# Split weights of `kv0` and of q0's plain blocks kept in DRAM and loaded split in the last quarter

## The chip, the cores and the metric

The kernel runs on one core of one Trainium2 chip. The metric is device time in microseconds (us) of one launch. Three runs of the kernel before the change took 2904.12 us in the median (2902.68 to 2905.22). About 0.2%, some 5.8 us, is what a measurement can tell from no change.

## What is computed

A trunk of two layers over 2048 tokens of width 1024, in float32. Layer A is a gated MLP whose gate mixes tokens inside chunks of 128. Layer B is attention with 24 query heads in three groups of dilation 1, 4 and 16; all read one set of keys and values that is projected from layer A's output. Cut to what the change touches:

```python
h = rms_norm(x, norm_g) * (1 + scale) + shift
k, v = jnp.split(h @ w_kv, 2, axis=-1)          # shared_kv, 6 heads of 128 each
...
qz = h @ w_in                                    # dilated_layer: 24 query heads and z
q = qz[..., :N_Q_HEADS * HEAD_DIM]; z = qz[..., N_Q_HEADS * HEAD_DIM:]
for g, (window, d) in enumerate(DILATED_GROUPS):
    o, lse = dilated_group_attn(q_g, k_g, v_g, slopes_g, window, d)
alpha = jax.nn.softmax(jnp.stack(lses), axis=0)
y = sum(alpha * outs) * jax.nn.silu(z)
return x + gate * (y @ w_out)
```

## The kernel before

The tokens run in four quarters of 512 (`Q` = 0 to 3 in the code). Each goes through layer A and then through `proj_B` (L1205), which projects keys and values in three column blocks (`kv2`, `kv1`, `kv0`) and queries and gate in blocks `q2`, `q1`, `q0`, `z`. Attention is written as generators that are interleaved with the projections as filler: group 2 (dilation 16) needs all tokens, so its 16 blocks run in quarter 4 beside `kv0`, `q1` and `q0`; the last blocks of groups 1 and 0 (blocks 12 to 15) run beside the last product with `w_out`. This product, `pf` (L1678 to L1680), makes 16 tiles of tokens times two halves, 24 matmuls each; its left operand `yb` is made by `prepare` and `make_yb` out of `og` (attention output) and `zt` (gate), both read back from DRAM.

Matmuls run in three terms. Each float32 weight `w` of 128 rows by 512 columns, called a unit, is split into a high and a low half, and the product is `a_hi w_hi + a_hi w_lo + a_lo w_hi` (`mm3`). A unit comes in one of two ways:

- `raw_unit` (L264) loads 256 KB into a buffer of the pool `rp` (six), and `split` makes the high half by an ACT copy (L260) and the low half by a DVE subtraction (L262), in a buffer of the pool `wp` (eight);
- `split_unit` (L273) loads 512 KB, already split, from DRAM straight into a `wp` buffer. Some weights are kept that way already: `wk1`, `wk2` for the even units of `kv1`, `kv2`.

A plain block of a q or z projection is 4 units. In `dense_s` (L536) a projection is seven products of half size, on the blocks "11", "21", "22" (plain columns of the weight) and "t1" to "t4" (sums and differences of blocks, made earlier and kept in `wt`); so each projection has 12 plain units and 16 of the other kind. `kv0` is an ordinary product of 8 units (`kv_units`, L289).

All DMAs are issued by SP in one row, in order, on eight lanes in rotation; an issue waits for the lane's DMA eight before. Stores are put into `pending` and issued by `flush` behind the next units' loads. A scheduler orders the instructions of every engine ahead of time, from its own estimate of times, so that a load or a split that is added or taken away changes the order elsewhere too. Each engine then runs its row strictly in that order.

At the tail, a local attention block `b` of group `g` goes through these steps: keys, values (`kv`, L1337 for the block before, L1338 for its own) and queries (`qt`) are loaded; `pk` and `pq` transpose keys and queries on PE (L1362, L1374); `kT` and `qT` are their copies in a high half (ACT, L1368, L1379) and a low half (DVE, L1369, L1380); `ps` are the scores (L1407 to L1409); DVE adds the bias and takes the maximum (`pr`, `stat`, L1413 to L1417); ACT takes exponentials (L1423); `pp` transposes them (L1465), `pT` is the copy, `po` the output (L1484).

Of the kernel before, what the change touches and what calls it, by code (L numbers as in the profile page):

```python
# [12 lines left out]
F32 = mybir.dt.float32  # L13
# [6 lines left out]
D = 1024  # L20
S = 2048
AW = 2048
NQ = 4
# [11 lines left out]
def trunk(ctx, tc, out, x, c, a_ada_w, a_ada_b, a_norm_g, a_w_in, a_sgu_g, a_w_spatial,  # L35
# [21 lines left out]
    dp = ctx.enter_context(tc.tile_pool(name="dp", bufs=1, space=bass.MemoryType.DRAM))  # L57
# [12 lines left out]

    wq = [dp.tile([D, 512], F32, name=f"wq{i}") for i in range(4)]
    wob = [dp.tile([2, D, 512], F32, name=f"wob{n}") for n in range(2)]
    wk2 = {n: dp.tile([512, 2, 512], F32, name=f"wk{n}") for n in (1, 2)}

    fillers = []
# [206 lines left out]
    def rows_of(t, k):  # L282
        return t[k * P:(k + 1) * P]
# [5 lines left out]
    def kv_units(Q, n, nm):  # L289

        saved = n and Q > 2 - n
        us = []
        for k in range(KT):
            if saved and k % 2 == 0:
                us.append(split_unit(rows_of(wk2[n], k // 2), f"{nm}{k}"))
                continue
            us.append(raw_unit(w_kv[k * P:(k + 1) * P, n * 512:(n + 1) * 512], f"{nm}{k}"))
            if n and Q == 2 - n and k % 2 == 0:
                nc.sync.dma_start(rows_of(wk2[n], k // 2), us[k].bitcast(F32))
        return us  # L300

    last_mm = [None]
# [216 lines left out]
    def v_blocks(b):  # L519

        n0 = AW + b * D
        src = {"11": (a_w_in, 0, n0), "21": (a_w_in, 4, n0), "22": (a_w_in, 4, n0 + 512)}
        src.update({f"t{i + 1}": (wv[b][i], 0, 0) for i in range(4)})
        return src, 4

    late_stores = []

# [677 lines left out]
    def proj_B(Q, hk, hb, keep, tail, ahead):  # L1205
# [41 lines left out]
        def q_block(g):  # L1247
            def ev(t, src, n):
                if t < 2 and n == 0:
                    c_ = sum_tile(f"qc{g}{Q}{t}")  # L1250
                    nc.scalar.activation(c_[:, 0:512], src, AF.Copy)
                    src = c_
                nm = f"q{g}{n}{Q}_{t}"
                sq = evt(f"hs_{nm}")
                nc.scalar.activation(sq, src[:, 0:512], AF.Square)
                nc.vector.tensor_reduce(src[:, 512:516], sq.rearrange("p (h d) -> p h d", d=P),
                                        AX.X, ALU.add)
                pending.append((qd[g][rows(t), n, 0:516], src[:, 0:516]))
            dense_s(hb, in_blocks(g), f"q{Q}{g}", ev)

        def z_block(**extra):
            def ev(t, src, n):
# [497 lines left out]
```

## Time and profile before

| what | value |
|---|---|
| median of three runs | 2904.12 us |
| the profiled execution | 2904.99 us, span 2903.3 us |
| granted TensorE clock, mean | 0.999 |
| PE busy | 2875.6 us, 99% of the span |
| DVE, ACT, POOL busy | 76%, 57%, 9% |
| DMA | 693.82 MB, mean 239 GB/s |

The page gives busy time by engine first, then the span in slices, the DMA queues, the chain that ended last and the costliest groups. The span is the time from the first to the last instruction of the profiled execution; 1.7 us of its own time lie around it. A group's line names code line, engine, operation and tiles, then busy time, mean duration in ns and the idle time ahead of it with what ended it. A timeline's row has the start, the length, the instruction, and in brackets the idle time before it and the engine and instruction that ended it. Matmuls are pipelined: a 128x512 matmul is listed with 0.39 us, but the next starts 0.23 us after it.

### The profile page before, as it was taken

The page shows a single profiled execution, that of the slowest core. Times are in us where ns is not written, and L with a number is a line of the kernel's source. Part 1 is how long each engine was busy: PE and PEld are TensorE (multiplying, and loading weights), DVE is VectorE, ACT ScalarE, POOL GpSimd, SP SyncE. Part 2 cuts the span into 40 slices and gives each one's busy share as a digit, 9 for nine tenths or more (in the row PEclk, how much of TensorE's full clock was granted, in tenths as well). Part 3 has the DMA queues.
Part 4 walks back from the last instruction along what each step waited for, and adds up shares of the span by engine and source line. Part 5 has one row for each costly group of instructions (what it writes and reads, how often), then busy time and mean ns, then how long its engine had stood idle before and what let it go on. Part 6 is the DMA issues. An engine that isn't in the chain of part 4 may idle for free. (4 is left out here: it accounts for less than half of the span.)

```text
span 2903.3 us, 44921 instructions
## 1 busy us (share of the span) xinstructions
PE 2875.6 (99%) x14610; PEld 2419.2 (83%) x14610; DVE 2219.1 (76%) x4246; ACT 1667.6 (57%) x3400; POOL 258.2 (9%) x549
## 2 busy tenths in 40 slices
PE   8999999999999999999999999999999999999999
PEld 5888888888888888888888888888888888988887
DVE  6786677787758986887878876987678876888972
ACT  4423345668456765676555665676355667876540
POOL 1000001101011000000010000000010003311100
PEclk9999999999999999999999999999999999999999
DMA  7899788777998577776676676766554667889842
GB/s 258 298 311 297 265 287 292 241 250 249 311 334 284 171 259 225 239 247 201 212 262 198 192 253 212 243 225 197 172 174 155 223 219 238 269 265 340 260 144 87
DMA packets 390783, 693.82 MB, mean 239 GB/s; under 512 B 42027, under 2 KB 119821, under 8 KB 390549
## 3 DMA queue, kind: packets, MB, share of 16 engines
q1 hardware_dynamic: 390548, 690.97, 72.3%
q8 instruction: 115, 1.88, 0.3%
q14 instruction: 120, 0.98, 0.1%
HBM read 530.97 MB, written 159.85 MB: 238 GB/s over the span
## 5 line engine op out<-in xcount | busy, mean ns | idle before, releaser
L306 PE MATMUL pd_kv<-w_kv,hkh 128*128 128x512 f32 x768 | 238.5, 391 | 0.3 <-DMA w_kv<-wk 0.2
L355 PE MATMUL pd_u<-hAh,w_u 128*128 128x512 f32 x512 | 207.8, 406 | 0.0
L355 PE MATMUL pd_z<-hAh,w_z 128*128 128x512 f32 x512 | 205.8, 402 | 0.0
L1423 ACT ACTIVATE pr<-pr,stat,rt 128x256 f32<-128x256 f32 (+1 forms) x320 | 177.4, 556 | 45.3 <-DVE stat L1420 30.0
L357 PE MATMUL pd_u<-hAh,w_u 128*128 128x512 f32 x512 | 200.6, 392 | 1.7 <-DVE w_u L262 1.7
L357 PE MATMUL pd_z<-hAh,w_z 128*128 128x512 f32 x512 | 200.4, 392 | 0.0
L356 PE MATMUL pd_u<-hAl,w_u 128*128 128x512 f32 x512 | 200.0, 391 | 0.0
L356 PE MATMUL pd_z<-hAl,w_z 128*128 128x512 f32 x512 | 199.8, 390 | 0.0
L306 PEld LDWEIGHTS pd_kv<-w_kv,hkh 128*128 128x128 f32 x768 | 143.3, 188 | 30.1 <-ACT w_kv L260 0.6
L1484 PEld LDWEIGHTS po<-kv,pT 128*128 128x128 f32 x1200 | 147.6, 191 | 7.4 <-ACT pT L1321 1.2
L1484 PE MATMUL po<-kv,pT 128*128 128x128 f32 x1200 | 149.8, 275 | 1.0 <-ACT pT L1321 1.0
L306 PE MATMUL pd_kv<-w_kv,hkl 128*128 128x512 f32 x384 | 149.8, 390 | 0.0
L1351 POOL TENSOR_SCALAR rt<-qt 128x4 f32<-128x4 f32 x96 | 26.8, 279 | 1311.9 <-DMA qt<-qd 724.7
L1413 DVE SCALAR_TENSOR_TENSOR pr<-dist,rt,ps 128x256 f32<-128x256 f32 (+1 forms) x320 | 124.7, 431 | 22.4 <-PE ps L1409 10.4
L260 ACT ACTIVATE w_u<-raw_u 128x512 fp32r<-128x512 f32 x96 | 59.5, 628 | 142.4 <-PE pd_u L357 95.2
L260 ACT ACTIVATE w_o<-raw_o 128x512 fp32r<-128x512 f32 x104 | 64.2, 628 | 96.4 <-PE pd_o L306 37.8
L260 ACT ACTIVATE w_q<-raw_q 128x512 fp32r<-128x512 f32 x144 | 88.6, 628 | 49.9 <-PE pd_kv L306 9.9
L357 PEld LDWEIGHTS pd_u<-hAh,w_u 128*128 128x128 f32 x512 | 96.1, 188 | 23.9 <-DVE w_u L262 2.9
L357 PEld LDWEIGHTS pd_z<-hAh,w_z 128*128 128x128 f32 x512 | 96.1, 188 | 21.0
L355 PEld LDWEIGHTS pd_u<-hAh,w_u 128*128 128x128 f32 x512 | 96.5, 188 | 18.4 <-issue 1.7
L356 PEld LDWEIGHTS pd_z<-hAl,w_z 128*128 128x128 f32 x512 | 96.5, 188 | 17.6
L355 PEld LDWEIGHTS pd_z<-hAh,w_z 128*128 128x128 f32 x512 | 96.4, 188 | 17.4
(866 smaller groups left out, 7944.8 us busy)
## 6 DMA issues: line engine op xcount, KB each, us to landing
raw_q<-in_b_w_in_dram SPq DMA_DIRECT2D x144, 256.0 KB, 3.8
w_z<-wuz SPq DMA_DIRECT2D x64, 512.0 KB, 4.3
raw_o<-in_a_w_out_dram SPq DMA_DIRECT2D x104, 256.0 KB, 3.5
qt<-qd SPq DMA_DIRECT2D x96, 258.0 KB, 3.6
raw_v<-in_a_w_in_dram SPq DMA_DIRECT2D x96, 256.0 KB, 4.0
raw_u<-in_a_w_in_dram SPq DMA_DIRECT2D x96, 256.0 KB, 5.3
od<-ot SPq DMA_DIRECT2D x96, 256.0 KB, 2.5
raw_kv<-in_w_kv_dram SPq DMA_DIRECT2D x76, 256.0 KB, 4.7
```

What stands on the lines that cost most here:

```text
L260: nc.scalar.activation(hi, src, AF.Copy)
L306: last_mm[0] = nc.tensor.matmul(pt, a, u[:, w, :], start=f, stop=e, skip_group_check=more)
L355: nc.tensor.matmul(pts[i], wh, hh[:, k, :], start=k == 0, stop=False)
L356: nc.tensor.matmul(pts[i], wh, hl[:, k, :], start=False, stop=False)
L357: nc.tensor.matmul(pts[i], wl, hh[:, k, :], start=False, stop=k == KT - 1)
L1351: nc.gpsimd.tensor_scalar(rt[:, 12:16], u["qt"][:, 512:516], 1.0 / P, EPS, ALU.mult, ALU.add)
L1413: nc.vector.scalar_tensor_tensor(pr[:, i, :], dist3[:, d0:d0 + w], u["rt"][:, h:h + 1], psc[:, i, :], ALU.mult, ALU.add)
L1423: nc.scalar.activation(pr[:, i, :], pr[:, i, :], AF.Exp, bias=mneg[:, i:i + 1], scale=u["rt"][:, h:h + 1], accum_out=lsum[:, i:i + 1])
L1484: nc.tensor.matmul(po[:, h * P:(h + 1) * P], u["pT"][h // hp][:, h % hp, j, :], u["kv"][:, j, kh, 1, :], start=j == 0, stop=j == nk - 1)
```

## The change

Two kinds of units of the last quarter get a split copy in DRAM. `wk0` holds the eight units of `kv0`: even units are stored in quarter 2, odd ones in quarter 3; even ones are loaded split in quarters 3 and 4, odd ones in quarter 4. `wq0` holds the three plain blocks of `q0`, four units each: "11" is stored in quarter 1, "21" in quarter 2, "22" in quarter 3, and all 12 are loaded split in quarter 4. That makes 20 stores of 512 KB, and 24 loads of 512 KB where there were loads of 256 KB with a split.

```diff
+    wk0 = dp.tile([D, 2, 512], F32, name="wk0")
+    wq0 = {b: dp.tile([512, 2, 512], F32, name=f"wq0{b}") for b in ("11", "21", "22")}
...
         for k in range(KT):
+            if n == 0 and Q > 1 + k % 2:
+                us.append(split_unit(rows_of(wk0, k), f"{nm}{k}"))
+                continue
             if saved and k % 2 == 0:
...
+            if n == 0 and Q == 1 + k % 2:
+                pending.append((rows_of(wk0, k), us[k].bitcast(F32)))
         return us
...
+    def q0_blocks(Q):
+
+        src, nk = in_blocks(0)
+        for i, name in enumerate(("11", "21", "22")):
+            w, k0, n0 = src[name]
+
+            def units(nm, i=i, name=name, w=w, k0=k0, n0=n0):
+                if Q == NQ - 1:
+                    return [split_unit(rows_of(wq0[name], k), f"{nm}{k}") for k in range(nk)]
+                us = wunits(w, k0, n0, nm, nk)
+                if Q == i:
+                    pending.extend((rows_of(wq0[name], k), us[k].bitcast(F32)) for k in range(nk))
+                return us
+            src[name] = units
+        return src, nk
...
-            dense_s(hb, in_blocks(g), f"q{Q}{g}", ev)
+            dense_s(hb, in_blocks(g) if g else q0_blocks(Q), f"q{Q}{g}", ev)
```

The code behind the change has 23 lines more ahead of it, so `L1361` of the changed kernel is `L1338` of the one before. The scheduler's order moves in places far from the edit. Two of them follow.

At the tail, on SP, around the load of the own half of block 12 of group 1 (`kv1_12`; `L1337` and `L1360` load the half of the block before). Before, it stands among the last loads of the weights `z3bt`, ahead of `wo`:

```order
L1337 DMA kv1_12_26308<-kvd_91 128x512 [waits DMAHW7_49,PE_49]
L267 DMA raw_z3bt1_1_26084<-wt3_0_115 128x512 [waits DMAHW0_49,DVE_49]
L267 DMA raw_z3bt1_2_26089<-wt3_0_115 128x512 [waits DMAHW1_49,DVE_49]
L1338 DMA kv1_12_26308<-kvd_91 128x512 [waits DMAHW2_49]
L267 DMA raw_z3bt1_3_26094<-wt3_0_115 128x512 [waits DMAHW3_49,DVE_49]
L1337 DMA kv1_13_26375<-kvd_91 128x512 [waits DMAHW4_49,DVE_49]
```

Now it stands behind the loads of tile 4's `og` and `zt`, which are the last of four tiles' loads, all behind `wo`:

```order
L1621 DMA og4_0_26249<-od0_95 128x1024 [waits DMAHW4_49,PE_49]
L1621 DMA og4_2_26251<-od2_97 128x1024 [waits DMAHW5_49,PE_49]
L1628 DMA zt4_0_26253<-zd_101 128x512 [waits DMAHW6_49,DVE_49]
L1628 DMA zt4_1_26254<-zd_101 128x512 [waits DMAHW7_49,DVE_49]
L1361 DMA kv1_12_26260<-kvd_91 128x512 [waits DMAHW0_49]
L1360 DMA kv1_13_26327<-kvd_91 128x512 [waits DMAHW1_49]
```

The half of the block before has kept its place among the `z3bt` loads; the own half has moved back by some 40 issues.

At the tail, on PE, where block 12's exponentials are transposed (`pp1_12`). Before, its transposes stand among the matmuls of `pf0_1`, the second half of tile 0, and `pk1_12` with the first scores stood ahead, among `pf0_0`:

```order
L1465 MATMUL pp1_12_00_26399<-ident_136,pr1_12_00_26343 128x128 x2
L1679 MATMUL pf0_1_26457<-wo11_26122,yb0_26233 128x512
L1680 MATMUL pf0_1_26457<-wo10_25997,yb0_26233 128x512
L1465 MATMUL pp1_12_00_26399<-ident_136,pr1_12_00_26343 128x128 x2
L1678 MATMUL pf0_1_26457<-wo10_25997,yb0_26233 128x512
L1679 MATMUL pf0_1_26457<-wo11_26122,yb0_26233 128x512
L1465 MATMUL pp1_12_01_26406<-ident_136,pr1_12_01_26357 128x128 x2
L1407 MATMUL ps1_12_10_26424<-kT1_12_26325,qT1_12_1_26390 128x256
```

Now the last matmuls of `pf0_1` come ahead of `pk1_12`, and scores and transposes follow one another:

```order
L1702 MATMUL pf0_1_26409<-wo11_26074,yb0_26185 128x512
L1703 MATMUL pf0_1_26409<-wo10_25949,yb0_26185 128x512
L1385 MATMUL pk1_12_26272<-ident_140,kv1_12_26260 128x128 x3
L1430 MATMUL ps1_12_00_26294<-kT1_12_26277,qT1_12_0_26285 128x256
L1430 MATMUL ps1_12_01_26308<-kT1_12_26277,qT1_12_0_26285 128x256
L1397 MATMUL pq1_12_1_26337<-ident_140,qt1_12_1_26265 128x128 x2
L1431 MATMUL ps1_12_00_26294<-kT1_12_26277,qT1_12_0_26285 128x256
L1432 MATMUL ps1_12_00_26294<-kT1_12_26277,qT1_12_0_26285 128x256
L1430 MATMUL ps1_12_00_26294<-kT1_12_26277,qT1_12_0_26285 128x256
```

and, five rows further on, the transposes of the exponentials:

```order
L1431 MATMUL ps1_12_01_26308<-kT1_12_26277,qT1_12_0_26285 128x256
L1432 MATMUL ps1_12_01_26308<-kT1_12_26277,qT1_12_0_26285 128x256
L1397 MATMUL pq1_12_1_26337<-ident_140,qt1_12_1_26265 128x128 x2
L1488 MATMUL pp1_12_00_26351<-ident_140,pr1_12_00_26295 128x128 x4
L1488 MATMUL pp1_12_01_26358<-ident_140,pr1_12_01_26309 128x128 x2
L1430 MATMUL ps1_12_10_26376<-kT1_12_26277,qT1_12_1_26342 128x256
```

What moved is the filler: all 24 matmuls of `pf0_1` now stand ahead of the chain from `pk1_12` to `pp1_12`, none between its steps.

On DVE the low half of `kT1_12`, which those scores need, stood right behind the two operations of tile 0's `yb`:

```order
L1641 TENSOR_TENSOR yb0_26233<-pyb0_0_26234,yb0_26233 128x512
L1641 TENSOR_TENSOR yb0_26233<-pyb0_1_26241,yb0_26233 128x512
L1369 TENSOR_TENSOR kT1_12_26325<-pk1_12_26320,kT1_12_26325 128x512
L1380 SCALAR_TENSOR_TENSOR qT1_12_0_26333<-pq1_12_0_26328,gqk_544,qT1_12_0_26333 128x512
L262 TENSOR_TENSOR w_z3b22_0_26187<-raw_z3b22_0_26188,w_z3b22_0_26187 128x512
L262 TENSOR_TENSOR w_z3b22_1_26192<-raw_z3b22_1_26193,w_z3b22_1_26192 128x512
```

Now it stands behind the preparation of tiles 1 to 4 (`og`, three operations in two halves a tile), whose last rows are these:

```order
L1708 TENSOR_TENSOR of0_0_26404<-pf0_0_26248,xr10_0_26244 128x512
L1641 TENSOR_TENSOR og3_0_26236<-og3_0_26236,zt3_0_26240 128x512
L1641 TENSOR_TENSOR og3_0_26236<-og3_0_26236,zt3_1_26241 128x512
L1564 TENSOR_TENSOR og4_2_26251<-og4_2_26251,wst_197 128x512 x2
L1640 TENSOR_TENSOR og4_0_26249<-og4_0_26249,og4_2_26251 128x512 x2
L1641 TENSOR_TENSOR og4_0_26249<-og4_0_26249,zt4_0_26253 128x512
L1641 TENSOR_TENSOR og4_0_26249<-og4_0_26249,zt4_1_26254 128x512
L1392 TENSOR_TENSOR kT1_12_26277<-pk1_12_26272,kT1_12_26277 128x512
```

It moved behind 24 of them and one `of`.

In quarter 2, on DVE, at the second product of the gate's projection (`z1b21`; `st_z1bu` takes the first products out of PSUM). Before, three low halves stand ahead of it:

```order
L262 TENSOR_TENSOR w_z1b21_0_11897<-raw_z1b21_0_11898,w_z1b21_0_11897 128x512
L262 TENSOR_TENSOR w_z1b21_1_11902<-raw_z1b21_1_11903,w_z1b21_1_11902 128x512
L262 TENSOR_TENSOR w_z1b21_2_11907<-raw_z1b21_2_11908,w_z1b21_2_11907 128x512
L578 TENSOR_TENSOR st_z1bu0_11835<-pd_z1bb0_11773,st_z1bu0_11835 128x512
L578 TENSOR_TENSOR st_z1bu1_11836<-pd_z1bb1_11774,st_z1bu1_11836 128x512
L262 TENSOR_TENSOR w_z1b21_3_11912<-raw_z1b21_3_11913,w_z1b21_3_11912 128x512
```

Now both evacuations stand ahead of all four:

```order
L601 TENSOR_TENSOR st_z1bu0_11851<-pd_z1bb0_11789,st_z1bu0_11851 128x512
L601 TENSOR_TENSOR st_z1bu1_11852<-pd_z1bb1_11790,st_z1bu1_11852 128x512
L264 TENSOR_TENSOR w_z1b21_0_11913<-raw_z1b21_0_11914,w_z1b21_0_11913 128x512
L264 TENSOR_TENSOR w_z1b21_1_11918<-raw_z1b21_1_11919,w_z1b21_1_11918 128x512
L264 TENSOR_TENSOR w_z1b21_2_11923<-raw_z1b21_2_11924,w_z1b21_2_11923 128x512
L264 TENSOR_TENSOR w_z1b21_3_11928<-raw_z1b21_3_11929,w_z1b21_3_11928 128x512
```

The splits of the next product have moved behind the two evacuations, and on PE the four matmuls that need only high halves (of `w_z1b21_0` and of the product after it) now stand ahead of the others.

## Rows read from the trace of the kernel before

**Rows 1.** The page's first part: busy time of each engine, share, instructions.
```profile
PE 2875.6 (99%) x14610; PEld 2419.2 (83%) x14610; DVE 2219.1 (76%) x4246; ACT 1667.6 (57%) x3400; POOL 258.2 (9%) x549
```

**Rows 2.** What PE waited for, whole run: us in total, times, longest.
```profile
PE pt_a L880 <- DVE x L874: 5.3, 3, 3.3
PE pva L126 <- DMA veca<-in_a_ada_b_dram: 5.0, 1, 5.0
...
PE pp L1465 <- ACT pr L1423: 1.6, 1, 1.6
PE pf L1680 <- DVE yb L1641: 1.4, 1, 1.4
```

**Rows 3.** By stretch: us of PE, PEld, DVE, ACT, POOL; clock, DMA share, GB/s.
```profile
2400.00:2450.00 50.00, 47.20 (x291) 40.01 (x290) 31.24 (x76) 32.61 (x90) 20.99 (x44) 1.00 0.63 198
...
2550.00:2600.00 50.00, 50.00 (x279) 43.38 (x278) 40.96 (x85) 36.58 (x91) 6.88 (x16) 1.00 0.80 261
2600.00:2650.00 50.00, 49.74 (x250) 41.41 (x248) 36.44 (x65) 32.96 (x73) 0.00 (x0) 1.00 0.98 363
...
2700.00:2750.00 50.00, 49.23 (x302) 42.78 (x301) 44.68 (x97) 24.37 (x70) 7.25 (x16) 1.00 0.80 263
```

**Rows 4.** Groups by line, whole run: busy us, mean ns, idle before.
```profile
L262 DVE TENSOR_TENSOR w_q<-raw_q,w_q 128x512 fp32r<-128x512 f32 x144 | 94.4, 685 | 18.6 <-ACT w_q L260 18.0
...
L260 ACT ACTIVATE w_q<-raw_q 128x512 fp32r<-128x512 f32 x144 | 88.6, 628 | 49.9 <-PE pd_kv L306 9.9 <-DMA raw_q<-in_b_w_in_dram 7.4 <-DVE w_q L262 6.6
```

**Rows 5.** PE in time, tail: start, us, instruction, idle before in brackets.
```profile
2624.73 1.03 PE L1638 MATMUL pyb<-ident,og 128*128 128x128 f32 x8
...
2629.25 0.73 PE L306 MATMUL pd_z3ba<-w_z3b,hob 128*128 128x512 f32 x2 [0.23 <-ACT w_z3b L260]
...
2630.41 5.18 PE L306 MATMUL pd_z3ba<-w_z3b,hob 128*128 128x512 f32 x22
```

**Rows 6.** Landing of the loads of `kv`, 2300 to 2600 us.
```profile
DMA to landing us min/median/max: 3.3/4.3/5.2
```

**Rows 7.** Landing of the loads of `zt`, 2640 to 2660 us.
```profile
DMA to landing us min/median/max: 5.6/6.0/6.4
```

**Rows 8.** DVE in time, quarter 2, start of z1.
```profile
1234.27 1.89 DVE L262 TENSOR_TENSOR w_z1b<-raw_z1b,w_z1b 128x512 fp32r<-128x512 f32 x3
1236.17 1.37 DVE L578 TENSOR_TENSOR st_z1bu<-pd_z1bb,st_z1bu 128x512 f32<-128x512 f32 x2
```

**Rows 9.** PE in time, quarter 2, start of z1.
```profile
1231.21 5.60 PE L306 MATMUL pd_z1bb<-w_z1bt,hob 128*128 128x512 f32 x24
```

**Rows 10.** SP's queue in time, tail: start and length of DMA issues.
```profile
2602.36 0.42 SPq L1338 DMA_DIRECT2D kv<-kvd  x1
...
2642.74 0.96 SPq L1605 DMA_DIRECT2D zt<-zd  x2
2644.05 0.32 SPq L1343 DMA_DIRECT2D qt<-qd  x1
```

**Rows 11.** DVE in time, tail.
```profile
2636.24 1.28 DVE L1541 TENSOR_TENSOR og<-og,wst 128x512 f32<-128x512 f32 x2
2637.44 1.28 DVE L1617 TENSOR_TENSOR og<-og,og 128x512 f32<-128x512 f32 x2
...
2639.85 1.26 DVE L1413 SCALAR_TENSOR_TENSOR pr<-dist,rt,ps 128x256 f32<-128x256 f32 x3
...
2642.01 0.15 DVE L1417 SCALAR_TENSOR_TENSOR stat<-rt 128x2 f32<-128x2 f32 x1
```

**Rows 12.** ACT in time, tail.
```profile
2642.24 1.28 ACT L1423 ACT_TABLE_LOAD   x1 [1.55 <-DVE stat L1417]
...
2645.30 0.59 ACT L1423 ACTIVATE pr<-pr,stat,rt 128x256 f32<-128x256 f32 x1
```

**Rows 13.** The same columns for ten us at the program's start.
```profile
20.00:30.00 10.00, 8.90 (x22) 4.28 (x21) 7.80 (x14) 0.81 (x1) 0.00 (x0) 0.66 1.08 356
```

**Rows 14.** PE in time, start of the program.
```profile
17.62 1.84 PE L890 MATMUL pc_a<-sc,aw 128*128 128x1 f32 x16
```

## The prediction

> **What bounds the kernel now.** The table of engines comes first: TensorE (PE) is busy 99% of the span, 2875.6 of 2903.3 us [rows 1], so 27.7 us are all that any change can take away without removing matmuls, and this one removes none. The list of what PE waits for comes next: the two longest, 5.3 and 5.0, lie at the program's start, and what quarter 4 and the tail hold is small: 1.6 us for the exponentials `pr` and 1.4 for the low half of `yb` [rows 2]. None of them is a split of a weight of kv0 or q0. The table by 50-us stretches says the same: PE has 47.20 us in 2400 to 2450, where kv0 of quarter 4 ends and the group-2 attention starts, 50.00 in 2550 to 2600, where q0's blocks run, and 49.74 in 2600 to 2650; DVE (VectorE) and ACT (ScalarE) are far from full there, 31 to 41 and 33 to 37 of 50 [rows 3]. So this kernel is bound by PE's instruction stream, and what counts is whether PE's in-order row of instructions still finds its operands ready.
>
> **What it removes.** 24 units lose their split: one ACT copy of 0.628 us and one DVE subtraction of 0.685 us each [rows 4], 15 and 16 us in all, 20 of the 24 in quarter 4 (8 of kv0, 12 of q0). Both engines have room in those stretches, and PE's waits there hang on the attention's chain and not on splits. I cost the removal at 0 on PE's path; what covers it is the idle time of ACT and DVE. At best a less busy ACT and DVE, with the GpSimd order in which `hr_k` now stands ahead of `rt`, shortens the 2.8 us that PE lacks in 2400 to 2450 [rows 3]: from -2.8 to 0, and I take **-0.7**, near the zero end, since the longest of the waits (1.6 on `pr`) is a chain of its own.
>
> **What it adds in traffic.** 20 stores of 512 KB and 24 loads that are 512 instead of 256 KB: 10.5 + 6.3 = 16.8 MB. A load in quarter 4 has a unit's time before it is wanted: eight units, each used by six 128x512 matmuls of 0.23 us (22 in 5.18 us [rows 5], 0.16 of it the last one's tail), last 11 us, against landings of 3.3 to 6.4 us for 256 KB [rows 6, 7]. Even at twice the longest landing, 12.8 us, the first unit would be late by 2 us. So 0 to +2, and I take **0**, because the DMA engines are at 0.63 and 0.80 where those loads run, not full [rows 3].
>
> **What it moves, quarter 2.** Four stores put ahead of loads on SyncE's queue (SP) turn an order on DVE: in before, three of the four splits `w_z1b` come ahead of the evacuation `st_z1bu` (1234.27 and 1236.17 [rows 8]); now both evacuations come first, and the second of them waits for the end of the product: 1231.21 + 5.60 = 1236.8 [rows 9]. It ends at 1237.5, and the first low half, 0.685 us [rows 4], at 1238.2. PE issues the next product from 1231.21 + 24 x 0.227 = 1236.65 on; it now runs the four matmuls that need only high halves first (0.9 us, to 1237.55), and then waits 0.65 us. 0 to +1.5, taken **+0.7**.
>
> **What it moves, the tail.** This is the term that decides. Block 12's own keys and values (`kv1_12`, second half) are issued at 2602.36 in before [rows 10]. Now their load stands on SP behind the loads of `wo`, `z3b22`, all `og` and `zt` of tiles 1 to 4 and the stores of `zb`: behind the `zt` pair at 2642.74, about where the load of `qt` stands at 2644.05 [rows 10]. So it is issued at 2643.2 to 2644.0, and with 3.3 to 6.4 us to land ([rows 6, 7]; I take 5) it is there at about 2648.5.
> When does PE ask for it? After `pyb0` at 2624.73 [rows 5] PE now runs 0.9 us of transposes, 24 matmuls of `pf0_0`, 24 of `z3ba`, 24 of `pf0_1`, each 0.228 us, and five more transposes of 0.1: 0.9 + 72 x 0.228 + 0.5 = 17.8, plus 0.3 of wait for the `z3b` split (0.23 in before [rows 5]), which gives 2642.8. There stand the three transposes `pk1_12`, and behind them block 12's whole front: scores, softmax, transposes. In before 48 of those 72 matmuls and more lay between the steps of this chain and hid it; now they are all ahead of it.
> What ends last is DVE. Its copy `kT1_12` (low half) now stands behind the preparation of tiles 1 to 4. Those are six operations of 0.60 us a tile (a pair is 1.28 long and the next begins 1.20 after it began [rows 11]), 3.6 us each, and one `of` of 0.6; the first starts at 2636.24, so DVE is through at 2636.24 + 14.4 + 0.6 = 2651.2. Tile 4's `zt` agrees with it: issued by 2643.2, landed after 6.0 [rows 7] at 2649.2, two operations more: 2650.5. The second bound is the lower one. `kT1_12`'s low half ends at 2651.9 (2650.5 to 2652.5).
> From there the chain is bare: five score matmuls 0.6; bias, maximum and `stat` 2.3 (2639.85 to 2642.16 [rows 11]); ACT's table load 1.28 and four exponentials, from 2642.24 to 2645.9 [rows 12], 3.7; the last transposes 0.3. Sum 6.9, so the last `pp` ends near 2658.8. Between 2642.8 and 2658.8 PE has three `pk`, 12 scores of 256 columns, each half of a 128x512 matmul, and 12 transposes `pq` and `pp`: some 3.2 us of work. Idle: 16.0 - 3.2 = **12.8** (11.5 if the table load runs early; 10.2 to 13.5 with the bounds above). Of before's tail waits the 1.4 on `yb` [rows 2] goes, since PE comes later to it, and a new wait of 0 to 3 for `yb1` and block 12's second half takes its place; I take **-1.4 + 1.0**. Later waits, of which 2700 to 2750 holds 0.77 [rows 3], may shrink by half, as DVE has tile 4's work behind it: **-0.4**, from -0.8 to 0. Nothing after that gives time back: PE is bound by its own stream up to the end.
>
> **The sum** against the profiled execution (2904.99, span 2903.3): -0.7 + 0 + 0.7 + 12.8 - 0.4 - 0.4 = +12.0. The median of the runs is 2904.12, 0.9 below the profiled one; the difference is put on the median: **2916**. With the terms' ends: -2.8 + 0 + 0 + 10.2 - 1.4 - 0.8 = +5.2 (2909) and 0 + 2 + 1.5 + 13.5 + 1.6 - 0 = +18.6 (2922.7); the likeliest case alone runs from 2909 to 2921.
>
> **Rivals.**
> A, no change that can be measured, 2905: the load lands before PE asks, and DVE takes `kT1_12` as soon as it is there. For it: SP has only issues ahead of it, and if the lanes and `zb` were quicker by 5 us the load would land at 2643.5. Then kT ends at 2645, the last `pp` at 2652, PE idles 9.2 - 3.2 = 6.0, and with -2.8 from quarter 4, -1.4 and -0.8 from the later waits it is +1.0. Against: DVE's 15 us of preparation stand ahead in its order and do not depend on the load.
> B, faster, 2899: the chain hides wholly and all of -2.8, -1.4 and -0.8 is gained: 2904.1 - 5.0 = 2899.1, still above the 2898.3 from which I call it faster; a chance is left for more than the sum knows. Against: the order of PE leaves nothing between the steps of the chain.
> [...]
> D, split loads come late, 2922 and above: transfers are at 0.80 in 2550 to 2600 [rows 3], and with stores and larger loads every unit of q0's three blocks could land late. 2 us at the first unit of each of two or three blocks, +4 to +6. Against: the cover of 11 us.
> That the change does not do what it says can be ruled out from the orders: 24 loads of split units and 20 stores are there, and the splits are gone.
>
> **How the numbers follow.** Forecast 0.46, A 0.25, C 0.20, D 0.05, B 0.04. About 0.2% (5.8 us) is what a measurement of this kernel can tell from no change, so faster is below 2898.3 and slower above 2909.9. Slower: 0.46 + 0.20 + 0.05, less 0.01 of the forecast's low end, 0.70. Same: A and that end, 0.26. Faster: B, 0.04. The range takes in the forecast's ends, C, and all of A but its lowest part: 2904 to 2923.
>
> **What would show it.** Right: PE's list of waits gains one of about 5 to 6 us on `kv` in `pk` near 2643 to 2649 and waits on `kT`, `pr` within 15 us behind it, about 12 in sum; kv0 and q0 of quarter 4 keep the same length within 1 us; PE idles 0.5 to 1 us near 1237.5. Wrong: no wait at `pk1_12`, DVE idle ahead of `kT1_12`, or PE waiting on the split loads themselves. [...] The forecast falls if the SP issue of the second half of `kv1_12` comes before 2638, or if DVE has tile 4 done before 2645.

## The result and the profile after

| what | before | after |
|---|---|---|
| median, runs taken together | 2904.16 us (6 runs) | 2927.27 us (6 runs, 2926.18 to 2930.53) |
| ratio | | 1.0079, 95% interval 1.0068 to 1.0089 |
| the profiled execution | 2904.99 us, span 2903.3 | 2927.69 us, span 2926.0 |
| DMA | 693.82 MB, mean 239 GB/s | 710.60 MB, mean 243 GB/s |

The change costs 23 us, about twice the 12 that were forecast, and 4 us above the range. The direction was right.

The first part of the page of the kernel after answers to [rows 1]:

```profile
PE 2886.5 (99%) x14610; PEld 2427.1 (83%) x14610; DVE 2207.2 (75%) x4222; ACT 1655.1 (57%) x3376; POOL 258.0 (9%) x549
```

PE has the same 14610 matmuls, and is busy for 10.9 us longer with them. Its idle time has grown too, from 27.7 to 39.5 us. So half of the loss is no wait at all: the same matmuls ran more slowly. ACT and DVE are each busy for 12 us less, and PE's list of waits before holds none on a split that went.

PE's list of waits, which answers to [rows 2] (total, times, longest):

```profile
PE pk L1385 <- DMA kv<-kvd: 8.9, 2, 6.7
PE pp L1488 <- ACT pr L1446: 5.5, 4, 3.3
...
PE pd_z1ba L313 <- DVE w_z1b L264: 2.0, 1, 2.0
```

The wait of 1.4 on `yb` [rows 2] is gone. To find where the 22.7 us between the two profiled executions arise, take the same matmul in both traces and subtract its starts. The shift is 2.9 us at 22 us, where both programs still run the same instructions, and between 2.6 and 3.4 up to 600; it rises by 3.9 at 638, in quarter 1, falls back in the waits that before has behind it, and is 2.9 at 1041. It is 8.2 at 1321, behind the z projection of quarter 2. It is 8.4 at 2627, at the head of the tail, and 22.5 at 2726; from there to the end it stays. So two places make up the loss of this execution: **quarter 2's z1 with 5.3 us** and **the tail with 14.1 us**. The 2.9 of the start belong to the execution: of the traces below, kv0_only has 3.1 at 22 us, the others -0.4 to 1.2 at 30. Its place is seen in PE's timeline of the kernel after, against [rows 14] for the same sixteen matmuls:

```profile
18.32 3.41 PE L913 MATMUL pc_a<-sc,aw 128*128 128x1 f32 x16
```

They take 3.41 us, in before 1.84, though both programs are the same up to there. The trace shows what goes with it: its first record of the granted clock, of 1.00, stands at 29.6 us here and at 17.1 in before. Ahead of the first record the clock column below shows 1.00 without a measurement.

In quarter 1 the rise is a wait of 2.17 us on a load of `kv`, and a granted clock of 0.50 behind it, from 641 to 644:

```profile
640.44 0.52 PE L1385 MATMUL pk<-ident,kv 128*128 128x128 f32 x2 [2.17 <-DMA kv<-kvd]
```

All six traced kernels that store q0's block "11" alone, and in full, in quarter 1 have this wait, with 1.6 to 3.0 us; the other traced kernels do not. How much of the rise later waits give back differs: all of it here, but in stores_only and after_A some 3 us are left at 1041.

**The tail.** Four timelines of the kernel after: PE, SP's queue, DVE, ACT (start, length, instruction, idle before it).

```profile
2651.88 0.39 PE L1703 MATMUL pf<-wo,yb 128*128 128x512 f32 x1
2658.96 0.90 PE L1385 MATMUL pk<-ident,kv 128*128 128x128 f32 x3 [6.69 <-DMA kv<-kvd]
2660.55 0.79 PE L1430 MATMUL ps<-kT,qT 128*128 128x256 f32 x2 [0.69 <-ACT kT L1391]
...
2662.42 0.41 PE L1432 MATMUL ps<-kT,qT 128*128 128x256 f32 x1
2662.63 0.41 PE L1431 MATMUL ps<-kT,qT 128*128 128x256 f32 x1
...
2667.59 1.86 PE L1488 MATMUL pp<-ident,pr 128*128 128x128 f32 x6 [3.27 <-ACT pr L1446]
```

```profile
2650.56 1.72 SPq L1628 DMA_DIRECT2D zt<-zd  x2
2652.41 0.34 SPq L1361 DMA_DIRECT2D kv<-kvd  x1
```

```profile
2659.32 1.29 DVE L1641 TENSOR_TENSOR og<-og,zt 128x512 f32<-128x512 f32 x2
2660.53 0.69 DVE L1392 TENSOR_TENSOR kT<-pk,kT 128x512 fp32r<-128x512 f32 x1
```

```profile
2665.55 1.28 ACT L1446 ACT_TABLE_LOAD   x1 [0.50 <-DVE stat L1440]
```

The load of block 12's own keys is issued at 2652.41 behind the `zt` pair and lands at 2659, 6.5 us later; DVE is through with the preparation of tile 4 at 2660.5 and takes `kT` then; PE stands still for 6.69, 0.69 and 3.27 us, 10.65 in all. One more thing is to be seen: two scores follow one another in 0.21 us, where they take 0.12 at a clock of 1.00 (after_busy, below). The next table shows what goes with it.

**The clock.** Stretches of 1 us of the kernel after, in the columns of [rows 3]; the third value from the end is the granted clock.

```profile
2652.00:2653.00 1.00, 0.27 (x2) 0.00 (x0) 1.00 (x3) 0.00 (x0) 0.00 (x0) 1.00 1.05 420
...
2654.00:2655.00 1.00, 0.00 (x0) 0.00 (x0) 1.00 (x3) 0.00 (x0) 0.00 (x0) 0.73 1.01 401
2655.00:2656.00 1.00, 0.00 (x0) 0.00 (x0) 0.97 (x2) 0.30 (x1) 0.00 (x0) 0.50 1.06 401
...
2663.00:2664.00 1.00, 1.00 (x7) 0.93 (x5) 0.87 (x3) 0.00 (x0) 0.00 (x0) 0.50 0.25 98
...
2665.00:2666.00 1.00, 0.00 (x0) 0.00 (x0) 1.00 (x4) 0.50 (x2) 0.00 (x0) 1.00 0.51 87
...
2669.00:2670.00 1.00, 1.00 (x6) 1.00 (x6) 0.67 (x2) 1.00 (x5) 0.54 (x2) 0.50 0.95 332
```

PE goes idle at 2652.3. The granted clock is 1.00 up to 2654, 0.73 in the next microsecond and 0.50 from 2655 to 2664; after the next wait it falls again, to 0.56 in 2668 and 0.50 from 2669 to 2671. It is at 0.50 from 641 to 644 and from 1232 to 1234 too. In before, 20 to 30 us was the only such stretch that the column shows [rows 13]. An estimate from the tables of 1-us stretches, PE's busy time times what the clock lacks: 1.6 + 1.7 + 2.3 + 1.6 = 7.2 us in the four places, of which the first is given back by 1041. With the start's 2.9 that is most of the 10.9 us by which PE is busier. It is time of PE's matmuls; where PE then waits for another engine, it is not all lost.

Behind the long waits of the tail (3.3 to 6.7 us here, in loads_only and before_late, 3.73 in after_busy) the clock is at 0.50 behind each; behind waits near 2 us half pace is seen in some executions, and right behind one wait not. before_kv12, which costs nothing, waits 1.95 at 2724, and behind it the scores follow one another in 0.21 us. At the place in quarter 1 stores_only waits 2.98, and the two transposes behind take 0.66 us; after_busy waits 2.36, and they take 0.41:

```profile
638.22 0.41 PE L1388 MATMUL pk<-ident,kv 128*128 128x128 f32 x2 [2.36 <-DMA kv<-kvd]
```

**Quarter 2.** The largest wait stands at the first product of z1; the prediction spoke of the second. Before, on PE and on DVE:

```profile
1224.88 2.89 PE L306 MATMUL pd_z1ba<-w_z1b,hob 128*128 128x512 f32 x12
```

```profile
1216.94 1.29 DVE L262 TENSOR_TENSOR w_z1b<-raw_z1b,w_z1b 128x512 fp32r<-128x512 f32 x2
```

And after:

```profile
1227.97 0.39 PE L313 MATMUL pd_z1ba<-w_z1b,hob 128*128 128x512 f32 x1
1230.34 4.38 PE L313 MATMUL pd_z1ba<-w_z1b,hob 128*128 128x512 f32 x11 [1.98 <-DVE w_z1b L264]
```

```profile
1229.60 0.68 DVE L264 TENSOR_TENSOR w_z1b<-raw_z1b,w_z1b 128x512 fp32r<-128x512 f32 x1
```

Before, DVE began two low halves 8 us ahead of the product; now it begins the first 1.6 us after PE has begun the product, and PE waits for it. Eleven matmuls then take 4.38 us where twelve took 2.89, with a granted clock of 0.50 from 1232 to 1234. The wait that the prediction priced, at the second product, is there too, behind the four matmuls that need only high halves:

```profile
1244.09 0.99 PE L313 MATMUL pd_z1bb<-w_z1bt,hob 128*128 128x512 f32 x2
1245.18 5.28 PE L313 MATMUL pd_z1ba<-w_z1b,hob 128*128 128x512 f32 x22
```

At 0.23 us a matmul the next would start at 1244.54; it starts 0.64 later, and 0.65 was forecast. The 5.3 are of this execution. In after_busy, after_kv12 and stores_only, which turn the order here in the same way, PE waits 0.7 to 0.9 at the first product, and the shift grows by 2.8 to 3.1 from 1041 to 1321; in stores_only the clock is at 1.00 there, from 1225 to 1251.

### The profile page after: what moved, and what is told of

Same layout as the page of the kernel before. It is cut to its first block, busy times and chain, and to the rows that moved or that the text cites. A ratio compares the mean times of both kernels' runs of the same rounds, so it can differ in the third digit from the quotient of the medians.

```text
span 2926.0 us, 44854 instructions
## 1 busy us (share of the span) xinstructions
PE 2886.5 (99%) x14610; PEld 2427.1 (83%) x14610; DVE 2207.2 (75%) x4222; ACT 1655.1 (57%) x3376; POOL 258.0 (9%) x549
## 2 busy tenths in 40 slices
DMA packets 393662, 710.60 MB, mean 243 GB/s; under 512 B 42346, under 2 KB 120140, under 8 KB 393428
## 5 line engine op out<-in xcount | busy, mean ns | idle before, releaser
L363 PEld LDWEIGHTS pd_u<-hAl,w_u 128*128 128x128 f32 x512 | 96.5, 189 | 16.9
```

Source lines behind the costliest of these rows:

```text
L363: nc.tensor.matmul(pts[i], wh, hl[:, k, :], start=False, stop=False)
```

## Experiments

Theory T, formed after the result: the time goes where the changed traffic lets the scheduler set another order, the stores in front of z1 and the loads of quarter 4 in the tail; the clock adds to each wait. R is in most cases the rival that the bytes themselves cost; in the last kernels T, as it had then been recast, is called O. The shift is always that against the profiled execution of before. Each ratio is to runs of before on the same chip, whose medians were 2904.2 to 2905.4.

### kv0 alone, stores alone, loads alone

**kv0_only** keeps the part in `kv_units` and drops that in `q0_blocks`.

```diff
-            dense_s(hb, in_blocks(g) if g else q0_blocks(Q), f"q{Q}{g}", ev)
+            dense_s(hb, in_blocks(g), f"q{Q}{g}", ev)
```

> Only the part on kv0: 8 stores and 12 split loads, q0 as before. In the scheduler's order of this kernel neither of the two disturbed places differs from before: on SP the own half of kv1_12 stands 9 rows ahead of the first load of wo, on PE 69 matmuls of 512 columns lie between pk1_12 and the last pp1_12, and on DVE three splits of the second z1 product stand ahead of st_z1bu. Theory T (the loss comes from the two reordered places, the tail +14 and quarter 2 +6, with the clock's fall in each): 2904, 2901 to 2907. Rival R (the loss comes from traffic and late split loads, in proportion to bytes): 8 of 20 stores and 12 of 24 loads are 7.3 of 16.8 MB, so +10, 2914.

2905.75 us, ratio 1.0001 (0.9992 to 1.0010). Eight stores and twelve loads of split units, 4 and 3 MB more traffic, cost nothing and gain nothing. PE's order is that of before row for row.

**stores_only** has all 20 stores and no split load.

```diff
-            if n == 0 and Q > 1 + k % 2:
-                us.append(split_unit(rows_of(wk0, k), f"{nm}{k}"))
-                continue
...
-                if Q == NQ - 1:
-                    return [split_unit(rows_of(wq0[name], k), f"{nm}{k}") for k in range(nk)]
```

> All 20 stores of the change are made, but quarters 3 and 4 load and split kv0 and q0 as before, so that the stored copies are not used. The order at the tail is that of before, the order at z1 of quarter 2 that of the change. Theory T: quarter 2 loses its 5.7 us and the tail nothing, 2910 (2907 to 2914). Rival R: 10.5 of 16.8 MB, +14, 2918.

2912.07, ratio 1.0020 (1.0011 to 1.0030). The tail's order is that of before, and the shift grows by 1.0 there, not by 14. The number is in T's range, its place only in part: of the shift of 7.8 at the end, quarter 2 has 2.8 and quarter 1 some 3, which T did not foresee.

**loads_only** has the split loads in the change's number and size, and no store; they read the copies of other weights (`wk2`), so its output is not the reference's.

```diff
-                us.append(split_unit(rows_of(wk0, k), f"{nm}{k}"))
+                us.append(split_unit(rows_of(wk2[1 + k % 2], k // 2), f"{nm}{k}"))
...
-            if n == 0 and Q == 1 + k % 2:
-                pending.append((rows_of(wk0, k), us[k].bitcast(F32)))
...
-                    return [split_unit(rows_of(wq0[name], k), f"{nm}{k}") for k in range(nk)]
+                    return [split_unit(rows_of(wk2[1 + i % 2], k), f"{nm}{k}") for k in range(nk)]
...
-                if Q == i:
-                    pending.extend((rows_of(wq0[name], k), us[k].bitcast(F32)) for k in range(nk))
```

> No stores are added; the 24 split loads of the change are made, but from the copies of kv1's and kv2's units, so that kv0 of quarters 3 and 4 and q0 of quarter 4 are multiplied with other weights than the reference's. The order at z1 of quarter 2 is that of before, the order at the tail that of the change (own half of kv1_12 31 rows behind the first wo, 72 matmuls ahead of pk1_12 and none in the chain). Theory T: the tail's loss of 13 to 14 us alone, 2918 (2915 to 2921). Rival R: 6.3 of 16.8 MB, +9, 2913.

2919.57, ratio 1.0045 (1.0030 to 1.0060). The waits of the tail are all here:

```profile
PE pk L1381 <- DMA kv<-kvd: 6.6, 1, 6.6
...
PE pp L1484 <- ACT pr L1442: 5.1, 3, 3.3
```

Stores cost some 6 us and loads some 13 to 14, together 19 to 21 of the 23; kv0's part taken by itself costs nothing.

### The tail: one load moved, or one load taken away

**before_late** is the kernel before, with the own half of `kv1_12` held back on SP until the `zt` loads of tile 4 are issued.

```diff
...
+        own = nc.sync.dma_start(kv[:, nk - 1, :], blk_rows(kvd, g, b)[:, g, :])
+        if (g, b) == (1, 12):
+            tc.add_manual_dep(own.ins, last_zt[0].ins.name, ...NoSync..., reason="late")
...
```

> The kernel before, with one order forced: the load of kv1_12's own half is queued on SP behind the last load of zt of tile 4. No weight is stored or loaded split that was not before. The scheduler then gives the tail the change's order: own half 31 rows behind the first wo, 72 matmuls of 512 columns ahead of pk1_12, none in the chain, preparation of tiles 1 to 4 ahead of kT1_12 on DVE. Theory T (order at the tail): 13 to 14 us over before, 2919 (2916 to 2922), waits of about 6.6 on kv and 3.3 on pr, and the clock at half behind them. Rival R (the change's transfers are what delays the tail): 2905 to 2909, since none are there.

2920.47 (2917.55 to 2921.78), ratio 1.0048 (1.0032 to 1.0063). The shift is 0.2 at 2627 and 14.5 at 2727, where the change has 14.1. Its waits:

```profile
PE pk L1366 <- DMA kv<-kvd: 6.7, 1, 6.7
PE pp L1469 <- ACT pr L1427: 5.8, 3, 3.9
```

Not one byte has been added. The place of one 256 KB load in SP's row, and the order that follows from it on PE and DVE, by themselves reproduce the whole loss of the tail.

**after_kv12** is the change with one 512 KB load for both halves of `kv1_12`, at the place of the first half.

```diff
+        if prev is not None and (g, b) == (1, 12):
+            n_, r_ = divmod(b, 4)
+            v_ = kvd.rearrange("(n i r) g w -> n r i g w", n=4, r=4)
+            nc.sync.dma_start(kv, v_[n_ - 1:n_ + 1, r_, :, g, :].rearrange("n i w -> i n w"))
+            return kv.rearrange("p b (h two d) -> p b h two d", h=2, two=2)
```

> The whole change, and both halves of kv1_12 (block 8's and block 12's keys and values) come in one DMA of 512 KB in place of two of 256 KB, so that the own half can't be put off. On SP that load now stands 5 rows ahead of the first wo, and on PE 63 matmuls of 512 columns lie between pk1_12 and the last pp1_12. Theory T: the tail's 14 us come back, the 6 of quarter 2 stay: 2913 (2909 to 2917), no wait on kv at pk1_12 near 2650, clock at 1.00 there. Rival R: nothing of weight changes, 2927.

2917.99 (2912.58 to 2924.89), ratio 1.0047 (1.0029 to 1.0065): 9 us of the 23 are back, less than the 14 that were expected, and with a wide scatter. The profiled execution is the fastest of these runs. In it the wait of 6.7 is gone and the clock is at 1.00 from 2636 to 2680, but PE's order in the tail is still not that of before, and waits remain:

```profile
PE pp L1493 <- ACT pr L1451: 3.5, 4, 1.5
...
PE pk L1390 <- DMA kv<-kvd: 1.6, 1, 1.6
...
PE ps L1435 <- DVE kT L1397: 1.1, 1, 1.1
PE pd_z3bb L313 <- ACT w_z3bt L262: 1.1, 1, 1.1
```

**before_kv12** puts the same five lines into the kernel before, as a control.

> The kernel before with both halves of kv1_12 in one load, nothing else: a control for the two kernels that have that load beside the change. Theory O: the load alone is worth nothing against before, 2904 (2902 to 2907), so what those kernels differ from before is the change's. Rival: the later first half costs or the single load gains 3 us or more, under 2901 or over 2908, and then the tail of after_kv12 (3.4 us) is the load's own doing.

2905.32, ratio 0.9999 (0.9990 to 1.0009). The single load by itself gains nothing in the kernel before, where PE's row stays as it was; what it gains in after_kv12 goes with the order that it changes there.

### The clock

**after_busy** is the change with 28 matmuls of 512 columns, whose result nobody reads, behind the last matmul of `pf0_1`, so that PE has work while it waits for `kv1_12`.

```diff
+                if (t, n) == (0, 1):
+                    dm = pst("dm", "d")
+                    for _ in range(BUSY):
+                        mm = nc.tensor.matmul(dm, yb[:, 0, 0, :], wh[:, 0, :], start=True, stop=True)
...
```

> The whole change, and 28 matmuls of 512 columns more on PE, between the last matmul of pf0_1 and the three transposes pk1_12 of the own half, into a PSUM buffer that nobody reads: 6.4 us of work in the 6.7 us in which PE waits there. All else in the order is the change's. Theory T (the granted clock falls because PE stands idle): the clock is 1.00 from 2650 to 2664, the 12 scores behind pk1_12 come every 0.12 us and not every 0.21, and the work added makes the kernel 2 us faster, 2925 (2923 to 2928); the second fall, behind the wait on pr, stays. Rival C2 (the clock falls for another cause, the load of all engines and DMA there): clock 0.50 as before and the time 2927 to 2930.

2930.65 (2925.90 to 2934.74), ratio 1.0089 (1.0069 to 1.0108). PE's timeline and three 1-us stretches:

```profile
2636.17 0.73 PE L315 MATMUL pd_z3ba<-w_z3b,hob 128*128 128x512 f32 x2 [1.71 <-ACT w_z3b L264]
...
2650.62 6.51 PE L1713 MATMUL dm<-wo,yb 128*128 128x512 f32 x28
2657.14 0.55 PE L1388 MATMUL pk<-ident,kv 128*128 128x128 f32 x3
...
2660.50 0.28 PE L1434 MATMUL ps<-kT,qT 128*128 128x256 f32 x1
2660.62 0.28 PE L1435 MATMUL ps<-kT,qT 128*128 128x256 f32 x1
...
2664.85 1.86 PE L1491 MATMUL pp<-ident,pr 128*128 128x128 f32 x6 [3.73 <-ACT pr L1449]
```

```profile
2660.00:2661.00 1.00, 1.00 (x10) 0.89 (x8) 0.59 (x2) 0.00 (x0) 0.84 (x3) 1.00 0.81 322
...
2665.00:2666.00 1.00, 1.00 (x4) 0.43 (x4) 0.58 (x1) 1.00 (x5) 0.00 (x0) 0.50 0.92 287
...
2671.00:2672.00 1.00, 1.00 (x9) 0.91 (x8) 1.00 (x4) 0.92 (x3) 0.00 (x0) 1.00 0.76 291
```

With the first gap filled the clock is at 1.00 in 2660, among the scores, which now follow one another in 0.12 us. So it was PE's idleness that lowered it here, as T has it, and not the load of the other engines and of DMA, which is still there (DMA 0.81 and DVE 0.59 in that microsecond). The second fall stays too, to 0.50 in 2665, behind the wait of 3.73 on `pr`. What T had wrong is the time: no 2 us are gained, and the expected 2925 lies only just outside the runs' span. From the first `pk` to the first `pp` it now takes 7.71 us, in the kernel after 8.63; so of the estimated 2.3 us the lower clock cost some 0.9 there and no more: from the last `pq` to the first `pp`, where the chain of DVE and ACT runs, it takes 4.11 us here and 3.89 in the kernel after. That was lost again ahead of it: PE waits 1.71 on a split of `z3b` at 2636, which is not in the list of the kernel after. Why this wait is longer here is open.

### The stores: where they stand, and how large they are

**after_A** is the change, with block "21" of q0 stored in quarter 3 instead of 2.

```diff
-                if Q == i:
+                if Q == (0, 2, 2)[i]:
```

> The whole change, but block 21 of q0 is stored in quarter 3, with block 22, and not in quarter 2. The order at z1 of quarter 2 is then that of before, the tail's that of the change. Theory T: the loss of quarter 2 comes back and that of the tail stays, 2922 (2919 to 2925); PE has no wait at pd_z1ba near 1230. Rival R (traffic): as many bytes as the change, 2927.

2927.66 (2923.26 to 2931.65), ratio 1.0073 (1.0054 to 1.0092). The time is that of rival R, and not T's. Quarter 2's loss is gone, as T has it, but quarter 3 has a new one: the shift goes from 5.5 to 9 at z2, 1866 to 1932. The loss went along with the stores.

**early_A** adds to that a place for both loads of `kv1_12` ahead of the loads of `wo`.

```diff
+    early = {}
...
-                    us[i]["kv"] = us[i + 1]["kv"] = att_kv(g, b, us[i]["ring"])
+                    us[i]["kv"] = us[i + 1]["kv"] = early.pop((g, b), None) or att_kv(g, b, us[i]["ring"])
...
-        yield {"hooks": {2: lambda: load_wo(1, 0), 4: lambda: load_wo(1, 1)}, "mid": opening}
+        yield {"hooks": {2: lambda: (early.update({(1, 12): att_kv(1, 12, False)}), load_wo(1, 0)), 4: lambda: load_wo(1, 1)}, "mid": opening}
```

> Both places repaired in the whole change: block 21 of q0 is stored in quarter 3, and the two loads of kv1_12 are written ahead of the loads of wo1 in the program, which puts them 12 rows ahead of the first wo on SP and leaves 63 matmuls of 512 columns in block 12's chain. All 20 stores and 24 split loads are there. Theory T: the loss is gone, and so is nearly all gain: 2905 (2901 to 2909), not clear of before. Rival R (traffic, late split loads): 2919 to 2927. Rival G (with the order repaired the 24 splits saved are worth something): below 2899.

2917.99 (2914.21 to 2920.37), ratio 1.0041 (1.0027 to 1.0055); 2905 was expected, so T as it then stood failed, and the time lies just under the 2919 to 2927 of R. The shift is near 0 from 900 to 1860, 4.4 at 2625 and 13 at 2727: z2 of quarter 3 and the tail each keep a loss of their own. In the tail, PE waits 1.07 and 1.21 in 2631 to 2634, and the clock is at 0.50 from 2634 to 2637.

**kv12_C** is after_kv12 with all twelve units of q0's three blocks stored in quarter 1.

```diff
-                if Q == i:
+                if Q == (0, 0, 0)[i]:
```

> The change with two edits: both halves of kv1_12 come with one load at the place of the first half (as in after_kv12), and all twelve split blocks of q0 are stored in quarter 1, none in quarters 2 and 3. Quarters 2 and 3 then stand in the order of before, quarter 2's first product of z1b included. Theory O (a store costs through the order of splits that it sits in, not through its bytes; quarter 1 has later PE waits of before, about 3 us between 634 and 982, to swallow it): no step at 1228 to 1253 or in quarter 3, the shift against before under 1.5 us at 2624; the tail costs the 3.4 us of after_kv12; 2908 (2905 to 2911). Rival B (a store costs by its traffic wherever it stands, some 6 us for all): the step moves into quarter 1 and is still there at 2624, 4 to 6 us; 2913 (2911 to 2918).

2917.80 (2916.64 to 2919.85), ratio 1.0048 (1.0035 to 1.0060). Quarters 2 and 3 have no step, as both expectations had it. But quarter 1 does not swallow the loss, which T had it do: the shift is 0.9 at 30 us and 6.9 at 2625. So the signs are those of rival B, with the time at the upper end of its range. The tail costs more than in after_kv12, where T had 3.4: the shift goes from 8.2 at 2600 to 14.1 at 2727. Why is open. Quarter 1's loss arises at the first product of z0, with the same face as in z1:

```profile
604.09 0.73 PE L313 MATMUL pd_z0bb<-w_z0b,hob 128*128 128x512 f32 x2 [2.06 <-ACT w_z0b L262]
605.62 4.11 PE L313 MATMUL pd_z0bb<-w_z0b,hob 128*128 128x512 f32 x10 [0.79 <-DVE w_z0b L264]
```

Ten matmuls take 4.11 us, with a granted clock of 0.50 from 606 to 608. So far a store costs wherever it stands in front of a z projection, which order and bytes both explain.

**stores_320** is there to tell these apart. It is stores_only with 320 of the 512 columns of each q0 block stored. With these bytes the scheduler leaves PE's row as in before, and DVE's and ACT's but for a few rows.

```diff
-                    pending.extend((rows_of(wq0[name], k), us[k].bitcast(F32)) for k in range(nk))
+                    pending.extend((rows_of(wq0[name], k)[:, :, 0:320], us[k].bitcast(F32)[:, :, 0:320]) for k in range(nk))
```

> stores_only with the twelve stores of q0's blocks cut to 320 of the 512 columns of each half: 320 KB each instead of 512 KB, the same number of DMAs at the same places. Nothing reads them, so the output is whole. With these bytes the scheduler leaves PE in the order of before row for row, ACT and DVE but for a few rows; in quarter 2 the splits of z1b stand as in before. Theory O (the stores cost through the order that moves with them): 2905 (2903 to 2907), no wait at the first product of z1b in quarter 2, shift against before at 1260 the same as at 1200 within 1 us. Rival B (they cost through their bytes: the DMA engines are busy for nearly all of the 10 us ahead of z1, so the weights of z1 come later by the bytes stored, 1.3 MB at some 390 GB/s, 3.4 us, where four full ones are 2.1 MB, 5.4 us, and cost some 4 to 6): 2908.5 (2907 to 2911), raw_z1b lands 3 us later against PE than before and PE waits on w_z1b at its first product.

2906.99 (2902.76 to 2909.74, 11 runs), ratio 1.0002 (0.9993 to 1.0011). No loss can be told from the noise: the interval reaches from 2 us below before to 3 above, and B's 2908.5 lies at its upper end. What speaks against B is the trace, where the shift is 0.2 at 1228 and at 1260. SP's queue and PE in front of z1:

```profile
1189.96 2.41 SPq L258 DMA_DIRECT2D wq<-w_q  x3
...
1209.54 6.39 SPq L269 DMA_DIRECT2D raw_z1b<-in_b_w_in_dram  x4
```

```profile
1225.11 2.89 PE L310 MATMUL pd_z1ba<-w_z1b,hob 128*128 128x512 f32 x12
```

z1's weights are issued at 1209.54, about 1 us later than in before, and PE runs its first product without a wait. In the kernel after, the first two were issued at 1217.56, some 6 us later against PE than in before. The row of before, then that of after:

```profile
1208.41 6.58 SPq L267 DMA_DIRECT2D raw_z1b<-in_b_w_in_dram  x4
```

```profile
1217.56 2.12 SPq L269 DMA_DIRECT2D raw_z1b<-in_b_w_in_dram  x2
```

Five eighths of the bytes of q0's stores, at the same places, cost at most some 3 us, and show no step, where the order stays. That order and not bytes sets the price of the full stores is likely by this, but not shown: full stores in the order of before were not run, since the scheduler takes the bytes into its order. So for the tail the cause is shown (before_late), for the stores it is in part argued.

## Why the prediction was wrong in size, step by step

- **What bounds the kernel; the removal; quarter 4.** Right. PE's 50-us stretches of kv0 and q0 in quarter 4 hold the same in after, taken 8 us later, as in [rows 3]: 47.33 and 50.00 against 47.20 and 50.00. Of the gain of 0.7 there is 0.13. What the 24 splits would bring in the order of before is not shown: no kernel has the whole change in that order.

```profile
2408.00:2458.00 50.00, 47.33 (x291) 40.09 (x290) 30.43 (x72) 31.46 (x86) 21.09 (x44) 1.00 0.71 229
2558.00:2608.00 50.00, 50.00 (x281) 43.38 (x280) 38.48 (x81) 34.04 (x90) 7.66 (x19) 1.00 0.81 256
```

- **Traffic and late split loads, 0; rival D.** Right: no wait of PE on a split load of q0 or kv0 is in the list of quarter 4, and kv0_only costs nothing.
- **The tail, +12.8 and waits of 0.4 + 0.4 less.** Right in its mechanism, and shown by before_late: 14.1, where 12.0 was forecast. That the sizes are so near is in part luck. PE stands idle for 10.65 us, not 12.8, and the lower clock, which stands in no term, makes up for part of it. PE asks for `kv` at 2643.9 (forecast 2642.8). Taken back by the 8.4 of shift, the load is issued at 2644.0 (forecast 2643.2 to 2644.0), PE has `kv` at 2650.5 (2648.5: it takes 6.5 to land, not 5), DVE ends `kT` at 2652.8 (2651.9), and the last `pp` ends at 2661.7 (2658.8). The last difference is the chain, 8.9 us instead of 6.9. It is here that the lower clock enters, with an estimated 2.3 + 1.6 us of PE's own.
- **Quarter 2, +0.7.** This step failed: the term, 0 to 1.5, measured 5.3. The prediction read the order at the second product, `z1b21`, alone and priced one wait on the two evacuations there. That wait came as forecast, with 0.64 us. But the first product's low halves had moved too, and its weights' loads on SP, 6 us later. PE waits 1.98 there, 0.57 at 1259, and has a lower clock from 1231 to 1235 (0.55, 0.50, 0.50, 0.74), which costs an estimated 1.7. In three other executions, with waits of 0.7 to 0.9 there, the place cost about 3, still twice the term's upper end; in one of them, stores_only, the clock is seen at 1.00.
- **Quarter 1.** Not foreseen: a wait of 2.2 us on `kv` near 640, a clock of 0.50 behind it. Waits that before had up to 982 took it back, so it is net nothing in this execution; in stores_only and after_A some 3 us of it stay, and in kv12_C a loss of the same kind at z0.
- **The clock, rival C.** C is the case that the granted clock falls in the tail, at 2920, 4 us over the forecast. Its price is an estimate: a mean of 0.66 over 10 us [rows 13] is (1 - 0.66) x 10 / 0.5 = 6.8 us at the 0.50 that before shows from 22 to 26; as much in the tail costs 3.4, and slower scores 0.6. The clock is the second step that failed: the sum and its ends hold the clock at nothing, and in the profiled execution PE's matmuls took an estimated 7.2 us longer by it, 5.6 of them in quarter 2 and the tail. C came true, and not only in the tail but in four places. I held it at 0.20 since the wait of 5.0 at the program's start [rows 2] shows no lower clock behind it. That reading failed: the clock's column says 1.00 for 10 to 20 us of before, but that is no reading, as the trace's first record of the clock stands at 17.1. Eight transposes take 1.97 us at 10.19 and 1.03 at 580.16, so they ran at about half pace behind that wait as well (rows below); whether the wait or the start itself is behind it can't be told. C's own figure, 2920, was still short, because it priced one gap and only the tail.
- **Idle stretches and the clock.** In the four places of the kernel after the clock is at 0.50 behind idle stretches of 2.0 to 6.7 us. But behind the 2.36 us of after_busy in quarter 1 the two transposes take 0.41 us, against 0.66 in stores_only, so half pace doesn't set in at once behind every stretch near 2 us. At the start the column of the clock doesn't show half pace, and the times of the matmuls do:
```profile
10.19 1.97 PE L880 MATMUL pt_a<-ident,x 128*128 128x128 f32 x8 [1.01 <-DVE x L874]
...
580.16 1.03 PE L756 MATMUL pt_a<-ident,x 128*128 128x128 f32 x8
```

- **The range.** Its upper end, 2923, added the ends of the terms without C. With quarter 2 at 5.3 and the tail at 14.1 the sum is 2904.1 + 19.4 = 2923.5; what is left, 3.8 us, is near the 2.9 that the profiled execution lost in its first 22 us, at matmuls that the change doesn't touch. Whether the other five runs lost as much there, or 5.3 in quarter 2, can't be seen, since they have no trace; what makes up the median is open by some us.

## What to carry to other kernels

Where a scheduler sets the order from its own estimate of times, price an edit of DMAs by walking all places where the order moved, each at its first product and on the loading queue, and not at the one place that a diff of orders shows most plainly. In a kernel whose matrix engine is 99% busy, count in matmuls at half pace behind every new wait of the size of the tail's here (3.3 to 6.7 us, each with a clock of 0.50 behind it), and take them as possible behind waits near 2 us. And before work is taken off engines, look whether anything waits for it: here 12 us less on each of ACT and DVE show no gain in any run.

## What the runs showed of the hardware

- The granted clock halves within a kernel whose PE is 99% busy: after PE went idle at 2652.3 it is 1.00 to 2654, 0.73 in the next microsecond and then 0.50, and 1.00 again in 2665, 6 us after work came back. With that gap filled with matmuls it is 1.00 in 2660, and it fell behind the next wait, of 3.73 us (after_busy). Behind a wait of 2.17 us it fell to 0.50 in after; behind 2.36 in after_busy, at the same place, the two transposes show no half pace (0.41 us, against 0.66 in stores_only).
- The granted clock in the profile can read 1.00 where the matmuls' own times say half pace, at the program's start, where the trace has no record of the clock yet: eight transposes in 1.97 us at 10.19, 1.03 later. How long PE is slow there differs between executions of the same instructions: the first record, of 1.00, stands at 17.1 us in before and at 29.6 in after, and 2.9 us lie between them.
- Added traffic isn't felt beyond the noise where PE's order stays: kv0_only (8 stores, 12 larger loads) and stores_320 (20 stores) have ratios of 1.0001 and 1.0002 to before.
